# Issuing the next inputs' casts and the side work behind a product's evictions instead of in front of them, in a two-layer decoder step

## The chip, the core and the metric

The kernel runs on one core of a Trainium2 chip. The metric is the device time of one execution in microseconds; the result is compared by the median of several runs. A core has a matrix engine (TensorE, PE in the profile, with its weight loads as PEld), three engines for element-wise work (VectorE is DVE, ScalarE is ACT, GpSimd is POOL) and a queue that mostly issues transfers (SyncE, SP). All five take their instructions from queues of their own, in order.

## The reference

One inference step of a small decoder of width 2048 with two layers, over 1024 prompt tokens and 8 sampled tokens. The first layer is a pooling mixer, the second a windowed attention; both end in a projection and a layer norm.

```
def pool_layer(x, prefix, pos, w_in, w_grp, scale, w_out, g_ln, b_ln):
    z = x @ w_in                                   # 2048 -> 4096
    u, gate = z[..., :D_POOL], z[..., D_POOL:]
    d, new_state = multiscale_pool(u, prefix, pos) # trailing means over 2, 4, 8, 16 rows, less u
    d = jnp.einsum('btgc,gce->btge', d.reshape(B, T, N_POOL_GROUPS, POOL_GROUP), w_grp)
    d = d.reshape(B, T, D_POOL) * scale
    y = (d * jax.nn.silu(gate)) @ w_out            # 2048 -> 2048
    return layer_norm(ALPHA * x + y, g_ln, b_ln), new_state

def attn_layer(x, pos, kb, vb, k_pos, q_pos, blocked, w_in, sinks, w_out, g_ln, b_ln):
    z = x @ w_in                                   # queries and gate, 2048 -> 4096
    q = rope_partial(z[..., :D_ATTN].reshape(B, T, N_HEADS, HEAD_DIM), pos)
    gate = z[..., D_ATTN:]
    ...
    o = attn_core(q, kb, vb, q_pos, k_pos, sinks).reshape(B, T, D_ATTN)
    y = (o * jax.nn.silu(gate)) @ w_out
    return layer_norm(ALPHA * x + y, g_ln, b_ln)
```

The keys and values of the second layer come from one projection `h @ w_kv` of the first layer's output, and are shared. The outputs are the two token arrays, the last 15 pooled rows, and the last 128 keys and values.

## The kernel before

**Tiles and parts.** The tokens are cut into two chunks of 512 and 520 (the sampled tokens ride in the second). Each chunk passes through four parts: the input projection of the pooling layer (`ai`), its output projection (`ao`), the key, value, query and gate projections with the attention (`bi`), and the last output projection (`bo`); the table `PHASES` gives the order. All data live on the core in 54 slots of 128 x 1040 numbers (`Mem`), which are handed out and returned while the program is written, oldest free slot first. A slot can be used whole or in two halves.

**The arithmetic.** Numbers are 32 bits wide. Each operand of a matmul is split into a high part (a cast, on ScalarE) and a low part (the difference, on DVE), and each product is taken as three: high by high (L661), high by low (L662), low by high (L663). Most matrix products use seven block products instead of eight, in a form with sums of blocks made beforehand.

**A step.** One block product is a step: `run` inside `seven` calls `begin`, issues 24 matmuls (eight tiles times three), notes what is to become of the result in `self.posts`, and calls `end`. The seven products of a pair go in the order `ORDER7 = (0, 2, 1, 5, 3, 4, 6)`, or in `ORDERL`, where two pairs alternate. They share three banks of accumulators, so a result has to be taken out of its bank before a later step writes there. The evictions are the functions `p0` to `p6`:

- `p0` (L609, ScalarE) writes the negative of one bank into another; `p2` (L618) and `p1` (L615) copy a bank to a slot, on ScalarE
- `p5` (L624 or an activation, L1181 by its line) copies a finished block, on ScalarE
- `p3` (L629) and `p4` (L634) subtract on DVE; `p6` (L641) copies on ScalarE
- after the seventh product a `done` function goes on with the finished tile; in the output projections it is the residual sum (L1287, DVE)

**What `begin` does.** It first calls `flush`, which issues the evictions of the step before. Then it loads weight tiles some steps ahead (L284, from the SP queue), casts them four steps ahead (L491, ScalarE), subtracts three steps ahead (L506, DVE), and makes sums of weight blocks (L343, DVE, with a store from POOL, L345). The distances are one less where few slots are free.

**What `end` does.** After the matmuls of a step it issues, in this order: products of the attention that are due (`self.pe`), the events of the step (`self.events`: pieces of pooling, of attention, of the running sums of the norm), then `x_tick`, then at most one piece of side work.

- `x_tick` prepares the input tiles of the next part: it loads them (L786), casts them (L796, ScalarE) and subtracts (L805, DVE). How much it does depends on how many slots are free and on when the tile is due.
- Side work comes from generators: `sum_gen` makes sums of weight blocks for the output projections (loads L432, additions L439, L443, L444, stores L445), `t_gen` makes sums of input blocks (L853 to L857), `ln_gen` makes the norm of a finished chunk while the next product runs (L931 to L934 for its reciprocal root, L1026 and L1029 for the scaling, products L910 that average over partitions). A piece is taken if enough slots are free (`self.room`) and at a rate set for each part (`self.every`).

Since every engine works through its queue in order, the order in which the program is written sets the order on each of them. A helper, `in_order`, fixes it for PE, DVE and ScalarE.

Of the kernel before, what the change touches and what calls it, by code (L numbers as in the profile page):

```python
# [94 lines left out]
class Slot:  # L95


    def __init__(self, mem, i, h, a):
        self.mem, self.i, self.h, self.a = mem, i, h, a
# [83 lines left out]
class Kern:  # L183
    def __init__(self, ctx, tc, io):
        self.tc, self.io = tc, io
        self.nc = tc.nc
        pool = lambda name, **kw: ctx.enter_context(tc.tile_pool(name=name, **kw))
        one = pool("one", bufs=1)
        self.smp = pool("smp", bufs=2)
        dram = pool("dram", bufs=1, space=bass.MemoryType.DRAM)  # L190
        self.psd = [pool(f"psd{i}", bufs=1, space=bass.MemoryType.PSUM) for i in range(3)]
        self.pso = pool("pso", bufs=1, space=bass.MemoryType.PSUM)
        self.four = None
        ctx.callback(self.use_four, None)
        self.prm = one.tile([P, N_PRM], F32, name="prm")
        self.cst = one.tile([P, N_CST], F32, name="cst")
        self.mki = one.tile([P, 64], U8, name="mki")
        self.jr = one.tile([P, P], F32R, name="jr")
        area = one.tile([P, NK * NST], F32, name="area")
        three = lambda a, b, c: area[:, a : a + b * c].rearrange("p (b c) -> p b c", b=b)  # L200
        self.carry = three(0, NK, NST)
        self.kdec, self.qd, self.sgd = three(0, 2, NDEC), three(16, NDEC, 8), three(80, 8, NDEC)
        self.flag = one.tile([P, 1], F32, name="flag")
        self.mem = Mem(pool("mem", bufs=1), NSLOT)
        self.n = 0
        self.i = self.e = self.lastO = self.turns = self.ring = 0
        self.posts, self.events, self.side = [], {}, []
        self.extra, self.on = None, False
        self.fresh = None
        self.ahead = 7, 4, 3  # L210
        dr = lambda n, s: dram.tile(s, F32, tag=n, name=n)
        self.Td, self.act, self.l_sq, self.l_sh = {}, {}, {}, {}
        for c, (_, T) in enumerate(CHUNKS):
            for n, k in (("x", "ai"), ("g", "ao"), ("h", "bi"), ("o", "bo")):
                if (k, c) in STRASSEN:
                    self.Td[n, c] = dr(f"t{n}{c}", [P, 8, 4, T // 2])
            self.act["x", c] = io[f"x{c}"]
            for n in ("g", "h", "o", "p"):
                self.act[n, c] = dr(f"{n}{c}", [P, NK, T])
        self.gbd = dram.tile([32, 2 * P], F32, tag="gbd", name="gbd")  # L220
        self.ws = {
            n: [dr(f"s{n}{q}", [P, 4, 1024]) for q in range(np_)]
            for n, np_ in (("wia", 16), ("woa", 8), ("wkv", 2), ("wib", 16), ("wob", 8))
        }
# [288 lines left out]
    def flush(self):  # L513
        todo, self.posts = self.posts, []
        for go in todo:
            go()

    def begin(self):
        self.flush()
        a, b, d = self.ahead if self.strassen else (5, 4, 3)  # L520
        free = lambda: len(self.mem.whole())
        self.load_to(self.e + min(a, 5))
        while self.loaded < min(self.e + a, len(self.stream)) and free() > 2:
            self.load_to(self.loaded + 1)
        self.prep_to(self.e + (d if free() > 1 else d - 1))
        self.cast_to(self.e + (b if free() > 1 else b - 1))
        self.make_to(self.e + (b if free() > 0 else b - 1) + (1 if self.strassen else 0))
        self.e += 1
        return self.hl.pop(self.e - 1)

    def end(self):

        if self.late and self.i > 6:
            self.late.pop(0)()
        while self.i in self.pe:
            todo = sorted(self.pe.pop(self.i), key=lambda x: x[0])
            todo[0][1]()
            if todo[1:]:
                self.pe.setdefault(self.i, []).extend(todo[1:])
        for go in self.events.pop(self.i, []):  # L540
            go()
        self.i += 1
        self.x_tick()
        room = len(self.mem.whole()) - 2 * len(self.xq)
        if self.extra and next(self.extra, 1):
            self.extra = None
        if self.side and int(self.i / self.every) != int((self.i - 1) / self.every) and room >= self.room:
            if next(self.side[0], 1):
                self.side.pop(0)
# [709 lines left out]
    def phase_out(self, c, res, nxt, last=None):  # L1259
# [55 lines left out]
        return pre, acc  # L1315

    def shifted(self, c, p, s, pre, acc, end):

        nc = self.nc
# [1180 lines left out]
```

## Time and profile before

| | us |
|---|---|
| median of 3 runs (2304.54 to 2308.23) | 2304.7 |
| the profiled execution | 2305.89 |
| its span, first to last instruction | 2304.1 |
| PE busy | 2283.5 |
| PE's weight loads busy | 2209.6 |
| DVE busy | 1902.1 |
| ScalarE busy | 1368.2 |
| POOL busy | 198.1 |
| granted clock of TensorE, mean | 0.999 |

In a row of the timeline stand the start, the length, the engine, the line of the kernel, the operation, what it writes and reads, its shape and count, and in square brackets how long the engine sat idle before it and what ended that wait. In a table of waits stand the engine and line that waited, what released it, the microseconds in total, the number of times, and the longest one. In a row of a stretch stand its bounds, its length, and for PE, PEld, DVE, ACT and POOL the busy time with the count of instructions, then the granted clock, the share of the transfer engines and GB/s. The letter m stands for a slot, pD, pO, pS for banks of accumulators.

Transfers move 654.58 MB, 284 GB/s in the mean.

### The profile page before, as it was taken

How to read it: one execution, taken by the hardware profiler on the slowest of the kernel's cores; microseconds unless marked ns; L12 is line 12 of the kernel's file. 1: busy time of each engine (PE TensorE's matmuls, PEld its weight loads, DVE VectorE, ACT ScalarE, POOL GpSimd, SP SyncE). 2: the span in 40 equal slices, each digit the busy share in tenths (PEclk: the TensorE clock that was granted, in tenths of full speed). 3: DMA queues.
4: the chain of work that ended last, by engine and by line, in shares of the span. 5: the costliest groups of instructions: out<-in, count | busy, mean ns of one | idle time of the engine just before them, and what ended most of it. 6: DMA issues, size and time to landing. Idle time of an engine off the chain costs nothing. (4 is left out here: it accounts for less than half of the span.)

```text
span 2304.1 us, 50417 instructions
## 1 busy us (share of the span) xinstructions
PE 2283.5 (99%) x20279; PEld 2209.6 (96%) x20279; DVE 1902.1 (83%) x2433; ACT 1368.2 (59%) x2533; POOL 198.1 (9%) x400
## 2 busy tenths in 40 slices
PE   9999999999999999999999999999999999999998
PEld 7899999999999999999889999999999999999998
DVE  8787889777878878988888888899776777888896
ACT  4444446544546546555466776785776678656565
POOL 0111110011010000000011111100000000010001
PEclk9999999999999999999999999999999999999999
DMA  8768789988989988999687667787686678799794
GB/s 292 243 233 296 262 298 364 328 306 289 309 306 313 350 286 305 338 389 351 230 305 255 230 231 248 256 291 233 223 255 229 218 225 306 250 364 383 254 347 172
DMA packets 248220, 654.58 MB, mean 284 GB/s; under 512 B 26385, under 2 KB 106033, under 8 KB 247985
## 3 DMA queue, kind: packets, MB, share of 16 engines
q1 hardware_dynamic: 204816, 494.67, 63.8%
q0 software_dynamic: 43168, 156.68, 17.6%
q8 instruction: 159, 2.61, 0.5%
q14 instruction: 77, 0.62, 0.1%
HBM read 464.54 MB, written 177.20 MB: 279 GB/s over the span
## 5 line engine op out<-in xcount | busy, mean ns | idle before, releaser
L661 PE MATMUL pD<-m,m 128*128 128x260 f32 (+1 forms) x4976 | 1409.1, 283 | 6.8 <-DVE m L629 3.0
L662 PE MATMUL pD<-m,m 128*128 128x260 f32 (+1 forms) x4976 | 1401.8, 282 | 0.0
L663 PE MATMUL pD<-m,m 128*128 128x260 f32 (+1 forms) x4976 | 1401.2, 282 | 0.6 <-DVE m L506 0.5
L661 PEld LDWEIGHTS pD<-m,m 128*128 128x128 f32 x4976 | 936.8, 188 | 12.1 <-issue 2.3
L663 PEld LDWEIGHTS pD<-m,m 128*128 128x128 f32 x4976 | 937.3, 188 | 1.1 <-DVE m L506 1.1
L662 PEld LDWEIGHTS pD<-m,m 128*128 128x128 f32 x4976 | 936.8, 188 | 0.5
L506 DVE TENSOR_TENSOR m<-m,m 128x1024 fp32r<-128x1024 f32 x684 | 827.6, 1218 | 76.7 <-ACT m L491 42.9
L491 ACT CAST m<-m 128x1024 fp32r<-128x1024 f32 x684 | 712.8, 1048 | 286.8 <-DVE m L343 86.4
L343 DVE TENSOR_TENSOR m<-m,m 128x1024 f32<-128x1024 f32 x120 | 146.6, 1222 | 10.2 <-DMA m<-in_wia 6.9
L805 DVE TENSOR_TENSOR m<-m,m 128x1024 fp32r<-128x1024 f32 (+1 forms) x118 | 144.2, 1225 | 5.9 <-ACT m L796 3.2
L641 ACT COPY m<-pD 128x260 f32<-128x260 f32 (+1 forms) x87 | 32.5, 374 | 188.5 <-PE pD L663 188.5
L796 ACT CAST m<-m 128x1024 fp32r<-128x1024 f32 (+1 forms) x118 | 123.8, 1054 | 4.4 <-DMA m<-in_x 2.4
L689 PE MATMUL pD<-m,m 128*128 128x512 f32 x288 | 114.3, 397 | 0.0
L691 PE MATMUL pD<-m,m 128*128 128x512 f32 x288 | 113.5, 394 | 0.0
L690 PE MATMUL pD<-m,m 128*128 128x512 f32 x288 | 113.2, 393 | 0.0
L629 DVE TENSOR_TENSOR m<-pD,m 128x260 f32<-128x260 f32 (+1 forms) x90 | 38.1, 423 | 74.9 <-PE pD L663 74.9
L1870 ACT ACTIVATE m<-m,sm 128x128 f32<-128x128 f32 x256 | 99.3, 390 | 0.0
L1892 ACT ACTIVATE m<-m,sm 128x128 f32<-128x128 f32 (+1 forms) x320 | 93.8, 373 | 0.0
L1133 PE MATMUL pD<-m,m 128*128 128x260 f32 (+1 forms) x528 | 91.4, 323 | 0.0
L1133 PEld LDWEIGHTS pD<-m,m 128*128 128x128 f32 x528 | 79.4, 188 | 8.2
L618 ACT COPY m<-pD 128x260 f32<-128x260 f32 (+1 forms) x90 | 33.6, 374 | 90.3 <-PE pD L663 90.2
L609 ACT ACTIVATE pD<-pD 128x260 f32<-128x260 f32 (+1 forms) x88 | 32.5, 369 | 78.2 <-PE pD L663 68.2
(257 smaller groups left out, 2187.4 us busy)
## 6 DMA issues: line engine op xcount, KB each, us to landing
m<-in_wib SPq DMA_DIRECT2D x132, 512.0 KB
m<-in_wia SPq DMA_DIRECT2D x122, 512.0 KB
swia<-m POOLq DMA_DIRECT2D x64, 512.0 KB, 5.0
m<-swia SPq DMA_DIRECT2D x64, 512.0 KB
m<-swoa SPq DMA_DIRECT2D x64, 512.0 KB
m<-swob SPq DMA_DIRECT2D x56, 512.0 KB
m<-in_wob SPq DMA_DIRECT2D x52, 512.0 KB
m<-in_woa SPq DMA_DIRECT2D x48, 512.0 KB
```

The lines of the kernel that those rows point to most:

```text
L343: self.nc.vector.tensor_add(s[out].a[:, :1024], s[x].a[:, :1024], s[y].a[:, :1024])
L491: self.nc.scalar.copy(hi.r[:, :1024], self.stream[self.cast].src().a[:, :1024])
L506: self.nc.vector.tensor_sub(lo.r[:, :1024], s.src().a[:, :1024], hi.a[:, :1024])
L661: nc.tensor.matmul(ps[:, :TH], wh[:, s], h, start=new and k == 0, stop=False, skip_group_check=on)
L662: nc.tensor.matmul(ps[:, :TH], wh[:, s], l, start=False, stop=False, skip_group_check=on)
L663: nc.tensor.matmul(ps[:, :TH], wl[:, s], h, start=False, stop=k == 7, skip_group_check=on)
L689: nc.tensor.matmul(ps[:], wh[:, s], h, start=par == 0 and k == 0, stop=False)
L690: nc.tensor.matmul(ps[:], wh[:, s], l, start=False, stop=False)
L691: nc.tensor.matmul(ps[:], wl[:, s], h, start=False, stop=par == 1 and k == 7)
L796: self.nc.scalar.copy(h.r[:, :n], s.a[:, :n])
L805: self.nc.vector.tensor_sub(l.r[:, :n], s.a[:, :n], h.a[:, :n])
L1133: nc.tensor.matmul(ps[:, : cs.stop - cs.start], ws[:, s], d[:, cs], start=f0 and k == 0, stop=l0 and k == 3,)
```

## The change

`end` no longer runs `x_tick` and the side work. It puts both on a list, `owed`, and `flush` works the list off after it has issued the evictions. Since `begin` calls `flush` first, the input casts and the side work of a step now stand behind the evictions of that step's product, and still in front of the next loads, casts and subtractions of weights. The counter of steps has the same value at both places. Where a part ends, what is owed is worked off after the settings of the next part are in force.

```
-        self.posts, self.events, self.side = [], {}, []
+        self.posts, self.events, self.side, self.owed = [], {}, [], []
...
     def flush(self):
         todo, self.posts = self.posts, []
         for go in todo:
             go()
+        while self.owed:
+            self.owed.pop(0)()
...
     def end(self):
...
         self.i += 1
-        self.x_tick()
+        self.owed += [self.x_tick, self.work]
+
+    def work(self):
         room = len(self.mem.whole()) - 2 * len(self.xq)
         if self.extra and next(self.extra, 1):
             self.extra = None
         if self.side and int(self.i / self.every) != int((self.i - 1) / self.every) and room >= self.room:
             if next(self.side[0], 1):
                 self.side.pop(0)
```

More of the change, by code (lines that the diff above doesn't have):

```diff
@@ L206, in __init__ @@
         self.i = self.e = self.lastO = self.turns = self.ring = 0
-        self.posts, self.events, self.side = [], {}, []
+        self.posts, self.events, self.side, self.owed = [], {}, [], []
         self.extra, self.on = None, False
@@ L516, in flush @@
             go()
+        while self.owed:
+            self.owed.pop(0)()
     def begin(self):
@@ L542, in end, with work @@
         self.i += 1
-        self.x_tick()
+        self.owed += [self.x_tick, self.work]
+    def work(self):
         room = len(self.mem.whole()) - 2 * len(self.xq)
```

## The prediction

> **What bounds the kernel now.** I read the page's busy times first, then the table of who waited for whom on TensorE (PE), then the timeline around each of those waits, and last the waits of VectorE (DVE).
>
> ```profile
> span 2304.1 us, 50417 instructions
> PE 2283.5 (99%) x20279; PEld 2209.6 (96%) x20279; DVE 1902.1 (83%) x2433; ACT 1368.2 (59%) x2533; POOL 198.1 (9%) x400
> PE pD L661 <- DVE m L629: 3.0, 3, 1.3
> PE pD L661 <- ACT pD L609: 1.7, 2, 1.3
> PE pD L661 <- ACT m L618: 1.5, 1, 1.5
> PE pD L661 <- ACT m L624: 0.6, 1, 0.6
> PE pD L663 <- DVE m L506: 0.5, 1, 0.5
> L805 DVE TENSOR_TENSOR m<-m,m 128x1024 fp32r<-128x1024 f32 (+1 forms) x118 | 144.2, 1225 | 5.9 <-ACT m L796 3.2 <-ACT m L1892 1.2 <-PE pD L691 0.7
> ```
>
> The reader is to see that PE is busy for 2283.5 of 2304.1 us. The 20.6 us left are all that a new order can win, start and end of the kernel included. What the edit can reach are the waits of a matmul (L661) for an eviction: 3.0 + 1.7 + 1.5 + 0.6 = 6.8 us in seven places, 0.3% of the time. That is the ceiling of the gain. A change within 0.2%, 4.6 us, is about what a measurement of this kernel cannot tell from none.
>
> **What the edit moves.** It removes and adds no instruction. Call E the evictions of a step's product, P the split of a coming weight tile (cast L491 on ScalarE, subtraction L506 on DVE), V the events of a step, and S what is moved: input casts and a piece of side work. An engine's queue reads E P V S E P V S now, and E S P V E S P V afterwards. So an eviction loses just the S that stood right in front of it. On an engine that is behind, a weight split keeps the same work in front of it, since E and S both preceded it already. On an engine that is ahead and idles in front of an eviction, S used to fill that idle time; now S runs after the eviction, and P and V after S.
>
> Counted out, S is: 118 subtractions L805 on DVE (1.23 us each, row above) with as many casts on ScalarE and their loads on SP; the weight sums (two SP loads, three DVE additions and one POOL store a piece); the transforms and norms (SP loads, DVE and ScalarE operations, the averaging products on PE, stores). On SP their loads keep their place ahead of the weight loads, and on POOL their stores pass only the stores that an eviction issues; POOL is 9% busy. I take both at nothing. What hides them is that loads are issued steps ahead. Where a moved load is given the slot that an eviction has only just released, it and the weight loads behind it on SP can be up to one step later, 24 matmuls at 0.12 us, 2.9 us. On PE the averaging products stay behind the same step's matmuls.
>
> Two smaller edits come with it. The tick after the last step of a part now runs with the next part's settings, so input loads can start one step, 2.9 us, sooner; and the count of free slots that S checks is taken after the evictions have claimed or returned theirs. Neither shows in this trace. The bounds are one step's worth either way, 2.9 us, at a boundary where something is late; I take zero, because PE waits for no L805 in the table of waits outside the start.
>
> **The seven places.** The first three:
>
> ```profile
> 345.40 1.23 DVE L805 TENSOR_TENSOR m<-m,m 128x1040 fp32r<-128x1040 f32 x1
> 347.12 0.36 PE L661 MATMUL pD<-m,m 128*128 128x256 f32 x1 [1.29 <-DVE m L629]
> ...
> 352.11 1.22 DVE L506 TENSOR_TENSOR m<-m,m 128x1024 fp32r<-128x1024 f32 x1
> 353.38 0.19 PEld L663 LDWEIGHTS pD<-m,m 128*128 128x128 f32 x1 [0.35 <-DVE m L506]
> ...
> 356.16 1.05 ACT L796 CAST m<-m 128x1040 fp32r<-128x1040 f32 x1
> 357.12 0.36 ACT L609 ACTIVATE pD<-pD 128x256 f32<-128x256 f32 x1
> 357.54 0.38 PE L661 MATMUL pD<-m,m 128*128 128x256 f32 x1 [1.27 <-ACT pD L609]
> ...
> 361.95 1.22 DVE L506 TENSOR_TENSOR m<-m,m 128x1024 fp32r<-128x1024 f32 x1
> 363.57 0.28 PE L663 MATMUL pD<-m,m 128*128 128x256 f32 x1
> ...
> 1238.53 1.22 DVE L805 TENSOR_TENSOR m<-m,m 128x1024 fp32r<-128x1024 f32 x1
> 1240.23 0.36 PE L661 MATMUL pD<-m,m 128*128 128x256 f32 x1 [0.41 <-DVE m L629]
> ```
>
> At 347 us a subtraction of S (1.23 us) stands in front of the eviction L629, and PE waits 1.29 us for it. The wait goes, all but 0.06 us. But what is late next is a weight split: at 353.38 PE already waits 0.35 us for L506, which runs in a queue without a gap, with the same work in front of it as before. PE gets there sooner and waits longer. Net: 0.
>
> At 357 us the input cast L796 (1.05 us on ScalarE) stands in front of L609; 1.05 of the 1.27 us go. Here L506 ends at 361.95 + 1.22 = 363.17 and its matmul starts at 363.57, a margin of 0.4 us. Net: 0.4, the rest is given back.
>
> At 1240 us the wait of 0.41 us goes: L805, 1.22 us, stands right in front. Nothing nearby takes it back. Net: 0.4.
>
> Two places have no S in front of the eviction; in front of L609 at 1276 us and of L618 at 1572 us stand:
>
> ```profile
> 1275.99 0.38 ACT L1870 ACTIVATE m<-m,sm 128x128 f32<-128x128 f32 x1
> ...
> 1571.25 0.36 ACT L1777 COPY m<-pO 32x256 f32<-32x256 f32 x1
> ```
>
> L1870 is the softmax and L1777 a copy of the decode values, both events. The 1.5 us of L618 and the rest of L609 stay. Net: 0.
>
> The last two lie near each other; the last row is the table of busy time for a stretch (PE, PEld, DVE, ACT, POOL):
>
> ```profile
> 2128.76 1.04 ACT L796 CAST m<-m 128x1040 fp32r<-128x1040 f32 x1
> 2130.13 0.39 PE L661 MATMUL pD<-m,m 128*128 128x260 f32 x1 [0.63 <-ACT m L624]
> ...
> 2166.47 1.24 DVE L1330 TENSOR_TENSOR m<-m,m 128x1040 f32<-128x1040 f32 x1 [3.26 <-ACT m L1326]
> ...
> 2175.13 0.69 DVE L934 SCALAR_TENSOR_TENSOR m<-m,m 128x512 f32<-128x512 f32 x1
> 2176.31 0.36 PE L661 MATMUL pD<-m,m 128*128 128x260 f32 x1 [1.26 <-DVE m L629]
> ...
> 2194.67 1.21 DVE L506 TENSOR_TENSOR m<-m,m 128x1024 fp32r<-128x1024 f32 x1
> 2196.80 0.28 PE L663 MATMUL pD<-m,m 128*128 128x260 f32 x1
> 2166.00:2236.00 70.00, 68.74 (x572) 68.48 (x572) 68.49 (x67) 45.50 (x65) 4.46 (x6) 1.00 0.91 322
> ```
>
> At 2130 us the cast L796 is S: 0.6 us go. The shift survives, because at 2166 DVE itself waits (3.26 us) for a copy of an averaging product that PE delivers, and so comes sooner too. At 2176 us a reciprocal root of the norm, ending in L934, is S in front of L629: 1.26 us go. But from 2166 to 2236 us DVE is busy 68.49 of 70 us, and the least margin of a weight split I found there is 2196.80 - (2194.67 + 1.21) = 0.92 us. So 0.9 of the 1.26 us are kept.
>
> Sum: 0 + 0.4 + 0.4 + 0 + 0 + 0.6 + 0.9 = 2.3 us. The profiled execution took 2305.9 us, of which 2304.1 are the span; the median of the three runs is 2304.7, 1.2 us less. The same 2.3 us come off each: 2303.6 for the profiled one, 2302.4 for the median, which I predict.
>
> The cost on the other side, S running behind an eviction for which an engine idles, is not in the sum. Upper bound: a whole S, 1.2 us and more, in each round of seven steps; lower bound: nothing, since the splits are made three steps ahead. I take nothing, because the only L506 that PE waited for at the third matmul of a product lost 0.5 us in the whole run, and that was behind a DVE with no idle time.
>
> **The rivals.**
>
> All of the ceiling. Every eviction wait goes and nothing takes it back: 2304.7 - 6.8 = 2297.9. For it: all seven have the same form. Against: the two at 1276 and 1571 us have no S in front, and the queue at 353 us is full. [...]
>
> No change. DVE, not the eviction, sets the pace in the crowded stretches, so every gain is given back as at 353 us, or the evictions moved were never urgent (seven waits in the whole run). Time: 2304.7, half a microsecond either way.
>
> Slower, by one mechanism: work that filled DVE's idle time in front of an eviction now runs behind it, and the weight split behind that is late. The place would be the stretch from 921 to 1037 us, the norm beside an output projection.
>
> ```profile
> 921.60:979.20 57.60, 56.75 (x469) 56.08 (x468) 54.36 (x60) 34.17 (x47) 2.13 (x4) 1.00 0.93 338
> DVE m L629 <- PE pD L663: 74.9, 47, 3.2
> DVE m L634 <- PE pD L663: 45.8, 35, 2.8
> ```
>
> DVE is busy 54.36 of 57.60 us there. A round of seven steps takes 20.2 us, so the stretch has 5.7 rounds; one S of 1.22 us pushed behind an eviction in each gives 5.7 x 1.22 = 7.0 us, less the 2.3 won: 2309.4. It decides where a split's margin is below 1.22 us and DVE still idles ahead of an eviction. For it: DVE does idle 74.9 + 45.8 us ahead of L629 and L634. Against: that is over the whole run, mostly where DVE has time; where it has none, it doesn't idle. [...]
>
> **How the numbers follow.** Forecast (a gain of 0.7 to 4.5 us): 0.48. All of the ceiling, or most of it: 0.13. No change within 0.7 us: 0.17. Slower by this mechanism or by a slot that comes free late: 0.22, of which 0.06 stay under 4.6 us. So faster 0.13, same 0.48 + 0.17 + 0.06 = 0.71, slower 0.16. The range leaves out about a tenth at each end: 2299.0, short of the ceiling, and 2308.8, short of the slow rival's 2309.4. The forecast's own range is 2300.2 to 2304.0.
>
> **What would show it.** The waits of L661 for L629, 3.0 us now, and for L624, 0.6, should be near zero; that for L609 falls from 1.7 to about 0.6; that for L618 stays near 1.5. The waits of L663 for L506 should grow from 0.5 to some 2 us or more, around 353, 363 and 2197 us. DVE's idle time ahead of L629 should grow. I am wrong if L663 waits for L506 in new places (above all 921 to 1037 us), if loads land later and L491 waits for them, or if new eviction waits arise where none stand now.

## The result, and the profile after

The changed kernel takes 2322.8 us (median of 6 runs, 2321.24 to 2324.38) against 2304.7 before: slower by 0.7%, ratio 1.0074 [1.0063, 1.0084]. The ratio is taken over the fast runs; one run of the kernel before that took 4520.59 us is not among them. Forecast were 2302.4 us and a range up to 2308.8. Its profiled execution took 2321.8 us, with a span of 2319.9.

From the page after, the span and the busy times, and from the table of who waited for whom the rows that answer to those of before (us in total, times, longest). In these rows every line of those behind `end` in the file stands 4 higher (L609 is L613 now, L618 L622, L629 L633, L661 L665, L663 L667); L491 and L506 keep their numbers.

```profile
span 2319.9 us, 50389 instructions
PE 2288.9 (99%) x20279; PEld 2213.9 (95%) x20279; DVE 1901.7 (82%) x2433; ACT 1367.3 (59%) x2533; POOL 196.8 (8%) x400
```

```profile
PE pD L665 <- ACT pD L613: 11.4, 4, 4.7
PE pD L667 <- DVE m L506: 2.6, 6, 0.6
PE pD L665 <- ACT m L622: 2.1, 1, 2.1
DVE m L633 <- PE pD L667: 82.9, 46, 3.2
```

The work is the same: as many matmuls, vector and scalar instructions, and the same busy time on DVE and ScalarE. PE is even "busier" by 5.4 us, though it has nothing more to do; that comes back below. The waits for DVE's eviction (3.0 us in three places) and for L624 (0.6) are gone, as the change means them to be. But the wait for the negated copy `p0` has grown from 1.7 us in two places to 11.4 in four, and the one for the weight split L506 from 0.5 us to 2.6 in six.

I set the start of each of the 686 products in the trace after against its start in the trace before. The difference, in us, at the ends of the stretches where it changes (the places are in the time of the trace before or, for the waits for `p0`, after; the last column is the first experiment below):

| start before | what happened since the row above | after | settings untouched |
|---|---|---|---|
| 342.8 | start | -0.25 | -0.34 |
| 369.0 | the places at 347 and 357 | -0.40 | -1.89 |
| 910.7 | | -0.22 | -1.30 |
| 1011.1 | output projection beside the norm | +1.87 | +1.97 |
| 1065.8 | a wait for `p0` at 1063 | +3.19 | +2.03 |
| 1270.5 | the place at 1240 | +3.47 | +1.74 |
| 1286.9 | a wait for `p0` at 1283 | +8.19 | +1.81 |
| 1480.0 | | +8.16 | +1.42 |
| 1503.7 | a wait for `p0` at 1501 | +15.54 | +1.43 |
| 1580.9 | the place at 1572 | +16.04 | +3.42 |
| 2111.9 | | +16.06 | +3.33 |
| 2182.2 | the places at 2130 and 2176 | +13.91 | +0.94 |
| 2280.9 | last product | +14.87 | +1.89 |

Three jumps, at 1063, 1283 and 1501 us, make 13.4 of the 14.9 us. Here are all four waits for `p0`, in the timeline after; the row ahead of L613 that matters each time is a weight cast L491:

```profile
351.17 1.04 ACT L800 CAST m<-m 128x1040 fp32r<-128x1040 f32 x1
354.92 1.05 ACT L491 CAST m<-m 128x1024 fp32r<-128x1024 f32 x1 [2.71 <-DVE m L809]
...
356.39 0.36 ACT L613 ACTIVATE pD<-pD 128x256 f32<-128x256 f32 x1
356.81 0.38 PE L665 MATMUL pD<-m,m 128*128 128x256 f32 x1 [2.44 <-ACT pD L613]
...
1061.71 1.05 ACT L491 CAST m<-m 128x1024 fp32r<-128x1024 f32 x1 [4.08 <-issue]
1062.66 0.37 ACT L613 ACTIVATE pD<-pD 128x260 f32<-128x260 f32 x1
1063.08 0.39 PE L665 MATMUL pD<-m,m 128*128 128x260 f32 x1 [1.07 <-ACT pD L613]
...
1280.35 1.04 ACT L491 CAST m<-m 128x1024 fp32r<-128x1024 f32 x1 [4.60 <-DMA to<-m]
...
1282.95 0.36 ACT L613 ACTIVATE pD<-pD 128x256 f32<-128x256 f32 x1
1283.37 0.39 PE L665 MATMUL pD<-m,m 128*128 128x256 f32 x1 [3.22 <-ACT pD L613]
...
1489.69 0.53 POOL L861 DMA_DIRECT2D to<-m  x1 [0.69 <-DVE m L638]
1498.52 1.04 ACT L491 CAST m<-m 128x1024 fp32r<-128x1024 f32 x1 [6.90 <-DMA to<-m]
...
1501.12 0.36 ACT L613 ACTIVATE pD<-pD 128x256 f32<-128x256 f32 x1
1501.53 0.58 PE L665 MATMUL pD<-m,m 128*128 128x256 f32 x1 [4.65 <-ACT pD L613]
```

The 2.44 + 1.07 + 3.22 + 4.65 us are the 11.4 of the table. Read the releaser in the cast's brackets. "DMA to<-m" is a store that reads a slot (m) and writes the transforms in memory (to). The cast reads nothing that a store delivers; it waits because the slot it is to write is still being read. At 1501 us the store was issued from POOL at 1489.69 and the cast could start at 1498.52. At 357 us it is the same with DVE as the reader: the cast got the slot that an input subtraction (L809) had just given back. At 1061 us the row names no releaser; by the program's order the cast's slot is one that a split L506 of the same step gives back. The weight cast itself is early, four steps ahead of its use, but behind it in ScalarE's queue stands the eviction that PE needs at once, at 1283 and 1501 us with pieces of the softmax between them.

So why did the program hand such slots out? The slots go by the order in which the program is written. Following that order in the two kernels gives two causes, both from the place where the owed work is run:

- `self.last` (the flag that the last products of a part have begun; `x_tick` then may go down to 3 free slots instead of 5 to 9) is set between `end` of one step and `begin` of the next. The owed `x_tick` runs behind it and so takes slots one step earlier: a subtraction and a cast at 351 us, a subtraction, a cast and two loads ahead of 1063, two loads ahead of 1501. The next weight cast, which used to get a slot whose last reader was done, gets one whose reader is not.
- At the seam near 1221 us the next part's inputs are entered in the list `xq` before the owed side work runs. The number of free slots less twice that list falls short, a piece of the norm is skipped, and its last pieces run in other steps than before. Slots are short at 1276 us.

These are causes read from the program's order. The experiments test them.

Last the clock. The rows are stretches behind the two longest waits (bounds, length, PE, PEld, DVE, ACT, POOL, granted clock, transfer share, GB/s):

```profile
1283.00:1288.00 5.00, 4.63 (x26) 4.63 (x27) 4.49 (x6) 4.03 (x13) 0.53 (x1) 0.66 0.72 283
1288.00:1293.00 5.00, 5.00 (x44) 5.00 (x44) 2.65 (x3) 4.81 (x13) 0.53 (x1) 1.00 0.73 214
1502.00:1508.00 6.00, 6.00 (x38) 6.00 (x38) 2.90 (x5) 4.53 (x14) 0.53 (x1) 0.67 1.07 354
1508.00:1514.00 6.00, 6.00 (x76) 5.75 (x75) 4.08 (x4) 6.00 (x13) 0.26 (x1) 1.00 0.89 335
```

PE is nearly full in the first and third row and gets through 26 and 38 matmuls instead of the 44 and 50 or more that such stretches hold. Their granted clocks, 0.66 and 0.67, are means: in the trace the clock is 0.50 from 1284.14 to 1287.55 us and from 1499.18 to 1506.00 us, and 1.00 around that. That is the extra busy time of the page: these two waits cost a second time. The wait of 2.44 us at 357 us did not; why is taken up with the last experiment.

### The profile page after: what moved, and what is told of

It is laid out like the page before. It is cut to its first block, busy times and chain, and to the rows that moved or that the text cites. A ratio compares the mean times of both kernels' runs of the same rounds, so it can differ in the third digit from the quotient of the medians.

```text
span 2319.9 us, 50389 instructions
## 1 busy us (share of the span) xinstructions
PE 2288.9 (99%) x20279; PEld 2213.9 (95%) x20279; DVE 1901.7 (82%) x2433; ACT 1367.3 (59%) x2533; POOL 196.8 (8%) x400
## 5 line engine op out<-in xcount | busy, mean ns | idle before, releaser
L665 PE MATMUL pD<-m,m 128*128 128x260 f32 (+1 forms) x4976 | 1411.5, 284 | 13.5 <-ACT pD L613 11.4
L667 PE MATMUL pD<-m,m 128*128 128x260 f32 (+1 forms) x4976 | 1404.2, 282 | 2.9 <-DVE m L506 2.6
L665 PEld LDWEIGHTS pD<-m,m 128*128 128x128 f32 x4976 | 938.7, 189 | 19.0 <-ACT pD L613 12.2
L667 PEld LDWEIGHTS pD<-m,m 128*128 128x128 f32 x4976 | 939.4, 189 | 4.8 <-DVE m L506 4.7
L506 DVE TENSOR_TENSOR m<-m,m 128x1024 fp32r<-128x1024 f32 x684 | 828.0, 1219 | 89.2 <-ACT m L491 49.3
L491 ACT CAST m<-m 128x1024 fp32r<-128x1024 f32 x684 | 712.1, 1048 | 305.7 <-DVE m L343 82.0
L809 DVE TENSOR_TENSOR m<-m,m 128x1024 fp32r<-128x1024 f32 (+1 forms) x118 | 144.2, 1225 | 8.3 <-ACT m L800 4.2
L633 DVE TENSOR_TENSOR m<-pD,m 128x260 f32<-128x260 f32 (+1 forms) x90 | 38.0, 422 | 83.1 <-PE pD L667 82.9
L622 ACT COPY m<-pD 128x260 f32<-128x260 f32 (+1 forms) x90 | 33.7, 374 | 86.3 <-PE pD L667 86.3
L613 ACT ACTIVATE pD<-pD 128x260 f32<-128x260 f32 (+1 forms) x88 | 32.4, 368 | 74.7 <-PE pD L667 62.7
```

Of the source, the lines that this page charges most:

```text
L491: self.nc.scalar.copy(hi.r[:, :1024], self.stream[self.cast].src().a[:, :1024])
L506: self.nc.vector.tensor_sub(lo.r[:, :1024], s.src().a[:, :1024], hi.a[:, :1024])
L665: nc.tensor.matmul(ps[:, :TH], wh[:, s], h, start=new and k == 0, stop=False, skip_group_check=on)
L667: nc.tensor.matmul(ps[:, :TH], wl[:, s], h, start=False, stop=k == 7, skip_group_check=on)
L809: self.nc.vector.tensor_sub(l.r[:, :n], s.a[:, :n], h.a[:, :n])
```

## The experiments

Two theories. *Settings*: the loss comes from owed work that meets other settings, takes other slots, and makes a weight cast wait. *Queue*: it comes from the new order on the engines, which is what the change is about and what the slower rival of the prediction said. The kernel before is timed beside each group of runs (2305.9, 2306.3 and 2305.5 us); ratios are against it.

**The order of the change, with the old settings** (a_flush_in_end). The evictions and the owed work are issued at the end of `end`, so evictions, owed work and weight splits follow each other as in the change, and no flag has moved.

```
         self.owed += [self.x_tick, self.work]
+        self.flush()
```

> The changed kernel, but the evictions and then the owed input casts and side work are issued at the end of the step's own function, before the next part changes any setting. Every engine keeps the changed order (eviction, then casts and side work, then the weight split); only the settings under which the casts and the side work decide are those of the ending part again. Settings theory (the loss comes from owed work that runs under the next part's settings, claims slots one step early or holds the norm back, so that a weight cast gets a slot whose store is still in flight and the eviction L613 stands behind that cast): the three waits for L613 at 1063, 1283 and 1502 us go, worth 1.2 + 4.6 + 7.3 = 13.1 us, so about 2309.7; the waits of L667 for L506 (2.6 us) stay. Queue theory (work that filled idle time in front of an eviction now runs behind it): nothing changes, 2322.8.

Measured: 2310.0 us, ratio 1.0023 [1.0013, 1.0033]. Its waits (L609 is L614, L618 L623, L663 L668 here):

```profile
PE pD L668 <- DVE m L506: 3.9, 9, 0.9
PE pD L666 <- ACT m L623: 2.1, 1, 2.1
PE pD L666 <- ACT pD L614: 0.9, 2, 0.5
```

The waits for `p0` fall from 11.4 to 0.9 us and the three jumps are gone (last column of the table). By the ratios the settings cost 1.0074 - 1.0023 = 0.0051, 11.8 us of some 17, and the order the other 5.3. By the traces it is 14.87 - 1.89 = 13.0 us for the settings and 1.9 for the order; but the traced execution of this kernel, 2308.4 us, is the lowest of nine.

**One early tick in the kernel before** (e_early_tick). The order is untouched; two loads are issued one step early, as in the changed kernel near 1488 us.

```
             self.last = p == ps[-1]
...
+            if self.last and c == 0:
+                self.x_tick()
```

> The kernel before, in its old order, with one call more of the input-cast function at one place: right after the flag for the last pair is set in the first strassen part of the attention (before step 442). It brings two input loads forward by one step and moves no eviction. Settings theory: the weight cast two steps on gets the slot of a transform whose store is in flight, PE waits about 4.8 us for the eviction L609 near 1490 us and some 2 us more go to a lower granted clock: 2304.7 + 7 = about 2312. Queue theory: 2304.7, the order of evictions is untouched.

Measured: 2311.5 us, ratio 1.0026 [1.0015, 1.0036]; in the trace the products fall back by 4.05 and 1.58 us at that place (the cast L491 waits 6.13 us "DMA to<-m") and by no more than 0.7 us anywhere else. Two loads, one step early, cost 5.6 us.

**The same early loads into other slots** (m_young_slot). While the extra tick runs, `Mem.full` gives the youngest free slot instead of the oldest, so the loads take the slots with stores in flight.

```
-        i = min(self.whole(), key=lambda i: max(self.f[i]))
+        i = (max if self.young else min)(self.whole(), key=lambda i: max(self.f[i]))
...
+                self.mem.young = True
                 self.x_tick()
+                self.mem.young = False
```

> As e_early_tick (the order of before, two input loads issued one step sooner near 1488 us), but these two loads are given the youngest free slots, those whose stores to memory are still in flight, so that the cast L491 of the next step gets a slot free since earlier. Slot theory: the 4 us wait for L609 behind that cast and the lower clock after it go, the loads themselves wait with time to spare: 2305.5 us, ratio 1.000. Rival (the two loads cost by their traffic, or by what they delay on the queue of SP): 2311 or more, ratio 1.0026.

The waits for `p0`, first of e_early_tick, then of m_young_slot (one line lower there):

```profile
PE pD L661 <- ACT pD L609: 5.6, 3, 3.9
```

```profile
PE pD L662 <- ACT pD L610: 1.7, 2, 1.3
```

1.7 us is the value of the kernel before. The wait hangs on which slot the cast gets, not on the loads. In the profiled execution (2305.6 us, the lowest of eleven) nothing is left of the loss; the median is 2307.9 against the 2305.5 expected, ratio 1.0010 [1.0001, 1.0019], so some 2 us of the median remain that this trace does not show. I leave them open.

**Half of the change each** (c_x_only, d_work_only). Only `x_tick` is owed, or only the side work.

```
-        self.owed += [self.x_tick, self.work]
+        self.owed += [self.x_tick]          # c; in d: self.x_tick(), and self.work owed
+        self.work()
```

> The changed kernel with only the input casts behind the evictions; the side work stays in front, as before. Settings theory: the waits for L613 near 1063 and 1500 us stay (1.2 + 7.3 us), the one near 1283 goes, the gains of about 0.5 at 1240 and 0.6 at 2130 us stay: about 2312. Queue theory: a share of the 18 us by the work moved (144 of some 330 us of VectorE work), some 8 us, spread over waits of matmuls for L506, none of them for L613 above 2 us.

Measured 2319.3 us, ratio 1.0062 [1.0047, 1.0078], 7 us more than expected. The falls at 1063 (1.5) and 1501 us (5.7) came where they were expected, the second 1.6 us smaller, and the one at 1283 us is gone. A further 4.5 us at 1597 us, where DVE waits 4.61 us for a transfer from slot to slot and PE 2.92 us for DVE, I had not foreseen. The traced execution (2316.3 us) is the lowest of four; the last 3 us of the median are not seen in it.

> The changed kernel with only the side work behind the evictions; the input casts stay in front, as before. Settings theory: the wait for L613 near 1283 us stays (4.6 us, of which 1.5 are lower clock), the ones near 1063 and 1500 go; the waits for L506 between 920 and 1010 us (2.6 us) stay and the gain of 1.3 at 2176 us stays: about 2310.5. Queue theory: some 10 us, spread over waits of matmuls for L506, none for L613 above 2 us.

Measured 2310.2 us, ratio 1.0020 [1.0011, 1.0030]. The time is as expected, but not its parts, as the traced execution shows them (2312.9 us, 2.7 above the median): at 1277 us it loses 1.2 us instead of 4.6, beside the norm 4.3. That the time fits is in part luck. At 1277 us a weight cast waits for a store here too (2.17 us, "DMA to<-m"), but PE's wait for `p0` is only 1.49 us and the clock stays 1.00.

**The free-slot count of the old part** (n_old_room). The changed kernel, except that a piece owed across a seam counts against the list of inputs as it was.

```
+        self.begun = self.i, len(self.xq)      # in x_begin, ahead of the new list
...
-        room = len(self.mem.whole()) - 2 * len(self.xq)
+        at, old = self.begun
+        room = len(self.mem.whole()) - 2 * (old if at == self.i else len(self.xq))
```

> The changed kernel, but a piece of side work that is owed across the end of a part counts the free slots against the inputs that were outstanding when its step ended, not against those of the next part. The norm's last pieces then keep the places they have in the kernel before. If the wait at 1283 us comes from their being skipped: it goes with its lower clock, 4.6 us, so 2318.2 us, ratio 1.0054; the waits for L609 at 1063 and 1501 us stay. Rival (that wait comes from the order of evictions and softmax on ScalarE): 2322.8.

Measured 2318.4 us, ratio 1.0056 [1.0043, 1.0068].

```profile
PE pD L667 <- ACT pD L615: 8.6, 4, 4.7
```

The jump at 1283 us is gone whole; those at 1063 (1.2) and 1501 us (6.8) stay. The time came as expected, though this trace loses 1.5 us at 360 us that the changed kernel's does not; why is taken up with the last experiment. So the count of free slots is needed for the jump at 1283 us, and one early tick is enough for most of the one at 1501 us. In d_work_only the same count without the early ticks cost 1.2 us. The jump at 1063 us was not tested by itself.

**The order alone: where it loses** (g_ao1_front, k_ao1_bi1_front). a_flush_in_end with S in front again in one part, or two.

```
-        self.owed += [self.x_tick, self.work]
+        if self.ph == "ao1":                # in k: self.ph in ("ao1", "bi1")
+            self.x_tick()
+            self.work()
+        else:
+            self.owed += [self.x_tick, self.work]
         self.flush()
```

> As a_flush_in_end (settings untouched, S behind the evictions), but in the output projection of the second chunk (931 to 1006 us) S runs in front of the evictions again. Queue theory: the 3.2 us that a_flush_in_end loses there come from the norm's scaling standing behind the residual sum L1287, so they go: about 2306.8 us, ratio 1.001, and the waits for L506 in that stretch go from 3.9 us to under 1. Rival (the loss comes from slots or loads, not from the order on DVE): 2310, the waits for L506 stay.

Measured 2306.8 us, ratio 1.0001 [0.9992, 1.0010]. The time is the one expected, but the kernel before took 2306.3 us beside it, not 2304.7, so that by the ratio nothing of the loss is left. Why the order costs there is seen on DVE, in the kernel before:

```profile
973.84 1.23 DVE L1029 TENSOR_TENSOR m<-m,m 128x1024 f32<-128x1024 f32 x1
974.98 1.23 DVE L1287 SCALAR_TENSOR_TENSOR m<-m,m 128x1040 f32<-128x1040 f32 x1
976.25 1.24 DVE L1301 TENSOR_TENSOR m<-m,m 128x1040 f32<-128x1040 f32 x1
977.41 1.22 DVE L506 TENSOR_TENSOR m<-m,m 128x1024 fp32r<-128x1024 f32 x1
```

and in the changed one:

```profile
974.22 1.24 DVE L1291 SCALAR_TENSOR_TENSOR m<-m,m 128x1040 f32<-128x1040 f32 x1 [0.27 <-ACT m L645]
975.49 1.24 DVE L1305 TENSOR_TENSOR m<-m,m 128x1040 f32<-128x1040 f32 x1
976.66 1.22 DVE L1030 TENSOR_TENSOR m<-m,m 128x1024 f32<-128x1024 f32 x1
977.91 1.22 DVE L1033 TENSOR_TENSOR m<-m,m 128x1024 f32<-128x1024 f32 x1
979.05 1.22 DVE L506 TENSOR_TENSOR m<-m,m 128x1024 fp32r<-128x1024 f32 x1
980.32 0.39 PE L667 MATMUL pD<-m,m 128*128 128x260 f32 x1 [0.56 <-DVE m L506]
```

Before, the norm's scaling (L1026, L1029) filled the time until the residual sum's input was there. After, DVE idles for that input, then scales, then splits the weights: L506 starts 1.6 us later, while the products at 974 us stand where they stood before (-0.1 us), and PE waits. Five of the six waits for L506 lie between 929 and 1005 us. With S in front there, the products hold their pace through that stretch (+0.5 us instead of +3.3 in a_flush_in_end), and the waits for L506 in the whole run fall from 3.9 us to 2.4, in that stretch from 2.5 us in five places to 1.0 in one (the kernel before has 0.5 at that one).

> As g_ao1_front, and in the part that begins at 1506 us (projections of the second chunk) S runs in front again too. If the 2.1 us that a_flush_in_end loses at 1572 to 1578 us come from the order there: 2304.7 us, ratio 1.000, as before. If they come from slots given out earlier: 2306.8, as g_ao1_front.

Measured 2307.7 us, ratio 1.0004 [0.9995, 1.0013]: no different from g_ao1_front. The 2.1 us at 1572 to 1578 are not lost in its trace, but others are, at 1178 (3.7), 1515 and 1691 us, the first at a place that this edit doesn't touch; the traced execution (2312.9 us) is the slowest of eleven. By the times it is inconclusive. The wait for the eviction `p2` at that place tells more: it is 1.52 us in the kernel before, 2.10 in a_flush_in_end, 2.14 in g_ao1_front and 1.54 here. So 0.6 us there come from the order in that part; what the other 1.5 us are is seen next.

**Only where it gained** (h_ai0_bo1_behind). As g_ao1_front, with S in front everywhere except in the first chunk's input projection and the last output projection (`self.ph not in ("ai0", "bo1")`).

> S behind the evictions only in the input projection of the first chunk and in the last output projection, where a_flush_in_end gained; in front everywhere else, settings untouched. If gains and losses are local: -1.5 us around 347 to 366 and -1.4 to -2 us around 2130 to 2176, so 2301.5 us, ratio 0.9986. If the gains are given back before the end, as the prediction had it for the first: 2303.5 or more.

Measured 2305.2 us beside 2306.3, ratio 0.9998 [0.9989, 1.0006]: no difference that the runs can tell. In its trace both gains are there and are kept to the end (-1.6 us behind 366, -2.5 behind 2176, -3.7 at the last product), but that execution (2302.8 us) is the lowest of eleven (up to 2310.9). A version that beats the kernel before is not shown.

**What a wait of PE costs** (l_stalls). In the kernel before, the eviction `p0` of six products is repeated.

```
-            nc.scalar.mul(B["b"][:, :TH], B["a"][:, :TH], -1.0)
+            for _ in range(1 + REPEAT.get(self.np0, 0)):        # 9, 11, 13, 15, 17, 19 times more
+                nc.scalar.mul(B["b"][:, :TH], B["a"][:, :TH], -1.0)
```

> The kernel before, in which the eviction L609 of six products, between 390 and 710 us where the granted clock is 1.00 throughout, is repeated 9, 11, 13, 15, 17 and 19 times more (0.37 us each, same values). TensorE should wait some 1.4, 2.1, 2.9, 3.6, 4.4 and 5.1 us. Clock theory: behind the waits above some 3 us the granted clock is 0.5 to 0.7 for about 5 us and costs 1.5 to 2 us more each; behind the shorter ones it is 1.00; span about 2304 + 19.5 + 5 = 2329. Rival (the lower clock in the changed kernel had another cause): 1.00 behind all six, span 2323.5.

The six waits (L661 and L609 are L664 and L612 here):

```profile
409.51 0.39 PE L664 MATMUL pD<-m,m 128*128 128x260 f32 x1 [1.20 <-ACT pD L612]
452.70 0.39 PE L664 MATMUL pD<-m,m 128*128 128x260 f32 x1 [2.02 <-ACT pD L612]
507.54 0.39 PE L664 MATMUL pD<-m,m 128*128 128x260 f32 x1 [2.78 <-ACT pD L612]
551.70 0.58 PE L664 MATMUL pD<-m,m 128*128 128x260 f32 x1 [3.63 <-ACT pD L612]
610.75 0.58 PE L664 MATMUL pD<-m,m 128*128 128x260 f32 x1 [4.46 <-ACT pD L612]
658.55 0.58 PE L664 MATMUL pD<-m,m 128*128 128x260 f32 x1 [5.27 <-ACT pD L612]
```

and the stretches behind the third, fourth and sixth:

```profile
507.00:513.00 6.00, 5.46 (x45) 5.46 (x46) 3.97 (x5) 4.48 (x8) 0.00 (x0) 1.00 0.75 242
551.80:557.00 5.20, 5.20 (x24) 5.20 (x25) 3.90 (x5) 2.02 (x3) 0.00 (x1) 0.50 0.40 130
658.70:663.70 5.00, 5.00 (x25) 5.00 (x26) 2.45 (x2) 1.98 (x3) 0.00 (x0) 0.56 0.38 116
```

Span 2333.8 us against 2304.1, and 2329 expected; 27.1 us of it behind these six places. Another 3.3 us come near 1691 us, where PE waits 1.77 us for DVE and the clock is 0.50 afterwards. Behind the waits of 1.20, 2.02 and 2.78 us the clock stays 1.00 and the next product takes its usual time. Behind 3.63, 4.46 and 5.27 us it is 0.50, and the next product takes 2.49, 2.15 and 2.16 us longer. The surcharge does not grow with the wait. In this run, then, a wait alone of 3.63 us and more was enough to lower the clock: these stretches have no softmax, and nothing else in them was changed.

Is there a length above which a wait does this? These six suggest one near 3 us, between 2.78 and 3.63, as do the 2.44 us (1.00) and 3.22 us (0.50) of the changed kernel, and the expectation had it so. The other traces do not bear it out. Here is a wait of 2.44 us for `p0` at 357 us twice, in the changed kernel and in n_old_room:

```profile
352.30:355.71 3.41, 2.07 (x18) 1.87 (x16) 3.34 (x5) 0.79 (x1) 0.00 (x0) 1.00 1.04 384
355.71:359.12 3.41, 2.31 (x19) 2.32 (x20) 2.91 (x4) 3.24 (x6) 0.00 (x0) 1.00 1.06 379
359.12:362.53 3.41, 3.41 (x31) 3.41 (x30) 3.38 (x4) 1.74 (x3) 0.53 (x1) 1.00 1.07 376
```

```profile
354.77:358.18 3.41, 1.07 (x9) 1.07 (x10) 2.91 (x4) 2.96 (x5) 0.00 (x0) 1.00 1.06 386
358.18:361.59 3.41, 3.41 (x19) 3.41 (x18) 3.38 (x4) 1.57 (x3) 0.13 (x1) 0.50 1.06 379
361.59:365.00 3.41, 3.41 (x30) 3.41 (x30) 3.41 (x4) 2.15 (x5) 0.40 (x1) 1.00 1.09 375
```

The stretches are not chosen freely. In the trace of the changed kernel the first record of the clock is at 4.14 us, and its changes at 1284.14, 1287.55, 1499.18 and 1506.00 us lie 375, 376, 438 and 440 times 3.413 us behind it. In that of the kernel before, the only change, at 2299.64 us, lies 672 times 3.413 us behind the first record at 5.88; in n_old_room the first record is at 6.61. So I cut the time of each trace into periods of 3.413 us from its first record; they lie elsewhere in each of these executions. In the changed kernel the wait fell across two periods, which left PE idle for 1.34 and 1.10 us of them, and the clock stayed. In n_old_room it fell into one, which left PE idle for 2.34 us, and the next period ran at 0.50: 1.5 us lost by the same wait. The wait of 2.78 us in l_stalls fell across two as well, PE was idle for 1.34 and 1.44 us of them, and the clock stayed 1.00:

```profile
502.69:506.10 3.41, 2.07 (x18) 1.85 (x16) 2.78 (x6) 3.16 (x9) 0.72 (x1) 1.00 0.75 216
506.10:509.52 3.42, 1.98 (x16) 1.98 (x17) 0.52 (x1) 3.33 (x8) 0.00 (x0) 1.00 0.93 266
```

And the wait for `p2` at 1572 us, 2.10 to 2.14 us long, lowered the clock in a_flush_in_end, d_work_only and g_ao1_front (idle 2.03, 1.98 and 2.14 us in one period) and not in the changed kernel (1.88) or in n_old_room (1.03 and 1.09). The 1.5 us left open above are this, and not the order.

## Why the prediction was wrong

**The step that failed** is "Two smaller edits come with it": the tick and the free-slot count under other settings, bounded at 2.9 us either way and taken as zero "because PE waits for no L805 in the table of waits outside the start". That looked at the wrong reader. The early tick was harmless to the input tiles; what it took was a slot, and the one who went without was the next weight cast. Two things were missing. I counted such an edit once "where a part ends", while `self.last` is set inside the parts as well, so there are more places. And I priced it by the step, 2.9 us, instead of by the longest reader of a slot, a store that held it 8.8 us at 1498. Against a_flush_in_end this term is 11.8 us by the times and 13.0 by the traces. The sentence nearest to it, a load "given the slot that an eviction has only just released", had the mechanism but named the wrong one who waits and the wrong releaser, and entered the sum as nothing.

**The second cost of the long waits** was in no term: at 1283 and 1501 us 1.5 and 2.1 us of the 4.7 and 7.4 us are the lower clock. How much of it a trace shows is in part chance, since it hung on where a wait fell: the 2.44 us at 357 us cost nothing more in the changed kernel and 1.5 us in n_old_room.

**The slower rival** was real, in its place and its mechanism, and mis-sized: 7.0 us forecast between 921 and 1037 us; 2.1 in the changed kernel, 3.3 in a_flush_in_end. It came behind L1291, the residual sum, not in every round of seven steps; that the other rounds had the margin I take from the waits that are missing there. To take its lower bound, nothing, for the sum was wrong; so was the reason that the waits for L506 were only 0.5 us, because those were the waits under the old order. The rows at 974 us show the mechanism: the split stands behind two scalings that stand behind a residual sum that waits 0.27 us, and starts at 979.05 us instead of 977.41.

**The gains** came, and some were larger than I took. At 2130 and 2176 us I kept 0.6 + 0.9 us; 2.15 came. At 1240 us 0.4 of 0.4. Of the 2.56 us of waits at 347 and 357 us I kept 0.4 and gave most of the rest back to L506; with the settings untouched 1.55 are kept (-0.34 to -1.89 in the table), so the queue of DVE "without a gap" was not the limit I made it. In the changed kernel the balance there is 0.15, near my 0.4, but for another reason: the wait at 357 us is 2.44 us, behind the cast that waits for L809.

**The list of what would show it.** Right: L629 and L624 vanish, DVE idles longer ahead of L633 (82.9 us, 74.9 before), L506 is waited for 2.6 us. Wrong: those waits lie in 929 to 1005 us, which I had named as the sign of the rival, and not at 353, 363 and 2197; L613 is 11.4 us, not 0.6; L622 is 2.1, not 1.5, by the order in that part (1.54 and 1.50 in the two versions that have S in front there).

**The sum** now, in the trace: settings 1.3 + 4.7 + 7.4 at the three jumps and 1.5 lost at 357, order 2.1 beside the norm and 0.5 at 1572, less the gains of about 4.1 (1.55, 0.4, 2.15), and about 1 at the last products: some 14 of the 14.9 us by which the last product is late. The rest is spread in steps below 0.5 us.

## What to carry to other kernels

A change that moves work past a point where flags or free counts change is two edits. Split them: replay the allocation and see which buffer each allocation gets, who reads that buffer last, and how long a store in flight holds it, before looking at the engines' order. Moving filler behind an eviction helped here where an engine was late (2.15 us at 2130 and 2176 us) and hurt where it idled (2.1 us beside the norm); in a kernel with both, it belongs, if anywhere, in the parts where the eviction's wait was seen; that this pays was not shown here (h_ai0_bo1_behind). And where PE waits for a few microseconds, a trace of one execution can show a surcharge by the clock that the next one does not (1.5 us and none behind the same 2.44 us); it is not to be booked on the edit.

## What the runs showed of the hardware

In the traces of the kernel before and of the changed kernel the granted clock of TensorE was 1.00 or 0.50, and it changed only at the edges of the periods of 3.413 us counted above, whose place differed (first records at 5.88 and 4.14 us). Up to the last products it went to 0.50 behind periods in which PE, at 1.00 so far, had been idle for 2.64 and 2.30 us (the changed kernel, periods that begin at 1280.72 and 1495.76 us), 2.34 us (n_old_room, 354.77 us), 2.03, 1.98 and 2.14 us (a_flush_in_end, d_work_only and g_ao1_front, the wait for `p2`) and 1.78 us (l_stalls, 1717 us). It stayed 1.00 behind periods with 1.88 us (the changed kernel, 1584.51 us), with 1.52 us (the kernel before, 1569.18 us), and behind the pairs with 1.34 and 1.10 us (the changed kernel, 352.30 us) and with 1.34 and 1.44 us (l_stalls, 502.69 us). No one length of idle time parts the two here: 1.78 us lowered the clock and 1.88 us did not. The waits that did it were 1.77 to 5.27 us long, and waits of 2.02, 2.12, 2.44 and 2.78 us that fell across two periods did not. The surcharge was 1.5 us where 0.50 lasted one period (1283 us in the changed kernel, 357 us in n_old_room), and 2.1 us (1501 us in the changed kernel) and 2.15 to 2.49 us (l_stalls) where it lasted two.

Behind the wait of 3.22 us the matmuls still started 0.11 to 0.13 us apart until 0.8 us after PE had resumed, at the end of the period (1284.14 us), and 0.21 us apart from there; behind 4.65 us in the changed kernel and 3.63 us and more in l_stalls the first was slow already (0.58 us long instead of 0.39): at 1501.53 us the clock had been 0.50 since 1499.18, within the wait.

A store of a 128 x 1024 slot, issued from POOL at 1489.69 us, still held its slot at 1498.5, 8.8 us on: three steps of PE.
